# Sample attention of a two-layer streaming encoder: probability rows ordered by batch, cached products of 64 columns, sink values picked by one-hot constants

## The chip, the cores and the metric

The kernel runs on one core of one Trainium2 chip. The metric is the device time in microseconds (us) of one execution of the whole program. The kernel before was run three times; the profile is of one further execution. Engines carry the profile's names: PE is the matrix engine (PEld its weight loads), DVE the vector engine, ACT the scalar engine, POOL the general-purpose one, and SP the one whose queue issues most of the DMAs.

## The reference

One step of an encoder of two layers. Layer 0 ("mixer A") attends to a sliding window of its own keys, with a distance penalty (ALiBi) and one learned "sink" value for each head; layer 1 ("mixer B") attends to shared keys and values with a learned bias by relative distance, and no sink. After each attention comes an MLP of width 4096 with a squared ReLU. There are 1024 prompt tokens, and 8 running streams ("batches") of 16 new tokens each, the sample: its tokens attend to a cache of 128 keys of their own batch, and to the 16 new tokens of their own batch. 16 heads of 64 elements share 4 key/value heads (kv heads), so 4 query heads go to each kv head. Everything is float32.

```python
def attend(q, k, v, bias, sink):
    b, tq = q.shape[:2]
    qg = q.reshape(b, tq, N_KV_HEADS, GROUP, HEAD_DIM)
    s = jnp.einsum('bqhgd,bkhd->bhgqk', qg, k).astype(jnp.float32) * (HEAD_DIM ** -0.5)
    s = s + bias.reshape(N_KV_HEADS, GROUP, tq, -1)
    if sink is None:
        p = jax.nn.softmax(s, axis=-1)
    else:
        sk = sink.astype(jnp.float32).reshape(N_KV_HEADS, GROUP, 1, 1)
        m = jnp.maximum(jnp.max(s, axis=-1, keepdims=True), sk)
        e = jnp.exp(s - m)
        p = e / (jnp.sum(e, axis=-1, keepdims=True) + jnp.exp(sk - m))
    o = jnp.einsum('bhgqk,bkhd->bqhgd', p.astype(v.dtype), v)
    return o.reshape(b, tq, N_HEADS * HEAD_DIM)
...
as_ = attend(qs, k_all, v_all, alibi_bias(pos_s, kpos_a, slopes), sink_a[i])  # sample, layer 0
hs = hs + as_ @ w_o_a[i]
...
as_ = attend(qs, kb_all, vb_all, relpos_bias(pos_s, kpos_b, rel_bias_b[j]), None)  # sample, layer 1
hs = hs + as_ @ w_o_b[j]
```

## The kernel before, in words

**Tiles and stages.** The prompt is 8 tiles of 128 tokens, and the 8 x 16 sample tokens are a ninth tile (ST). Each layer runs as attention, output projection, up projection, down projection. On the profile of before these are, roughly: attention A and its output projection from 0 to 460 us, the MLP of layer 0 to 1150, attention B and its output projection to 1660, the MLP of layer 1 to the end. Most large products are made of three matmuls on a high and a low part of each operand (lines 147 to 149, 186 to 188, 715 to 717: the same operation three times).

**What sets the order.** The program is written as generators that are woven together (`weave`), and a scheduler then lays out each engine's instructions by a model of their lengths and dependences. So an edit in one place can move instructions in others. Each engine works its own list in order; an instruction that waits holds up all behind it. SP's DMAs take eight semaphores in rotation (DMAHW0 to DMAHW7): a DMA waits for the landing of the one that stands eight before it in the queue, as the waits in the order rows below show.

**The sample's attention.** `unit` (L506 to L590) does it for two batches (`bp`, 4 pairs) and one kv head (`j`, 4): 16 units in each layer, 32 in all, stepped at its `yield`s between pieces of the prompt's attention. A unit loads the caches (`kc` L509, `vc` L511), turns the keys (`ps_utr`, L544, copied by L545), forms scores for 128 rows (4 heads x 2 batches x 16 tokens, ordered head, batch, token) over 256 cached and 32 new columns, and exponentiates them. A row needs only the 128 cached columns of its own batch; the 128 of the other batch are masked by the bias, so their probabilities are zero. Then:
- ACT scales the 256 cached columns by 1/sum in place (L570, tile `sp` in layer A, `ub` in layer B) and the 32 new ones into `pn` (L571), a tile with 128 columns, zero elsewhere.
- PE turns three blocks of 128x128 (L574, L575 and L576 for `pn`, into `ps_utp`), and ACT copies all three to `pts` (L578).
- PE forms `ps_uo` = values x probabilities with 128 columns each: L582 and L583 for the two caches, L584 for the new tokens' values. These are plain float32 products, each of which stands as two instructions on PE.
- ACT copies `ps_uo` out in two halves (L587), and a DMA stores them.

`q_stage2` (L211) lays out the queries: for ST in the row order of the units. `prep_bias` (L1100) lays out layer B's biases for the units in the same row order, and `shape_constants` (L48) the constants of layer A, made on the host and passed in as `consts` (`cst`, 596 columns).

**The sinks.** `sinks` (L1239) runs at the start: it loads `cst` (L1242) and the sinks broadcast to all partitions (`sink` L1244, 128x16), forms `usink` from them (L1246, L1247), and then loads `ssink`, 128 rows x 4 kv heads, by four DMAs (L1251), each of which fetches 4 single elements, 4 apart, for 32 partitions. `ssink` and `susink`, made from it, are read first by the units of layer A.

**The start.** Weights of the first projection (`w_qkv_a`) come in pieces called `raw`, 128x2x512, through L129 in `load_block`; POOL (L156) and DVE (L159) split a piece into its high and low part `w`. PE's first projections (L186 to L188) follow them, and ACT (L245, L252, L253) and DVE (L246) empty their banks.

Of the kernel before, what the change touches and what calls it, by code (L numbers as in the profile page):

```python
# [8 lines left out]
F32 = mybir.dt.float32  # L9
# [7 lines left out]
P = 128  # L17
# [26 lines left out]
C_SLS = 592  # L44
C_W = 596


def shape_constants():  # L48
# [9 lines left out]
    for hh in range(4):  # L58
        for b in range(2):
            r = slice(hh * 32 + b * 16, hh * 32 + b * 16 + 16)  # L60
            sa[r, b * P : (b + 1) * P] = P + i[:, None] - np.arange(P)[None, :]
            sa[r, 256 + b * 16 : 256 + b * 16 + 16] = np.abs(i[:, None] - i[None, :])
# [4 lines left out]
    c[:, C_ISL : C_ISL + H] = 1.0 / s  # L67
    c[:, C_SLS : C_SLS + KV] = s.reshape(KV, G).T[np.arange(P) // 32]
    return c
# [6 lines left out]
class Build:  # L76
# [134 lines left out]
    def q_stage2(self, qpool, qr, t):  # L211
        pt = self.transpose_pairs(qr, 4)
        qT = qpool.tile([P, 2, G, P], F32R, tag="qT", name="qT", bufs=2)
        if t == ST:
            for j in range(2):
                src = pt[:, 2 * j : 2 * j + 2, :].rearrange("p h (b q) -> p h b q", b=4)
                dst = qT[:, j].rearrange("p h q -> p (h q)")
                dst = dst.rearrange("p (b h q) -> p h b q", b=4, h=G)
                self.stack(src, dst[:, 0::2], dst[:, 1::2])
        else:  # L220
            dst = qT.rearrange("p j h q -> p (j h) q")
            self.stack(pt, dst[:, 0::2], dst[:, 1::2])
        return [qT[:, 0], qT[:, 1]]
# [282 lines left out]
    def unit(self, up, small, layer, bp, j, v8, gq8, cache_k, cache_v):  # L506
# [58 lines left out]
        else:  # L565
# [3 lines left out]
            self.mark = nc.vector.reciprocal(li, l)  # L569
        nc.scalar.activation(p[:, 0:256], p[:, 0:256], AF.Copy, scale=li)  # L570
        nc.scalar.activation(pn[:, bp * 32 : bp * 32 + 32], p[:, 256:288], AF.Copy, scale=li)  # L571
        yield
        pt2 = self.psum("u", [P, 3, P], "ps_utp")
        nc.tensor.transpose(pt2[:, 0, :], p[:, 0:128], self.ident)  # L574
        nc.tensor.transpose(pt2[:, 1, :], p[:, 128:256], self.ident)  # L575
        nc.tensor.transpose(pt2[:, 2, :], pn, self.ident)  # L576
        pts = up.tile([P, 3, P], F32, tag="pts", name="pts")
        nc.scalar.copy(pts, pt2)  # L578
        yield
        po = self.psum("u", [64, 2, 2, 32], "ps_uo")  # L580
        pof = po.rearrange("p a b q -> p (a b q)")
        nc.tensor.matmul(pof, vc[:, 0, :], pts[:, 0, :], start=True, stop=False)  # L582
        nc.tensor.matmul(pof, vc[:, 1, :], pts[:, 1, :], start=False, stop=False)  # L583
        nc.tensor.matmul(pof, v8[:, j * HD : j * HD + HD], pts[:, 2, :], start=False, stop=True)  # L584
        so = up.tile([P, 2, 32], F32, tag="so", name="so")
        for par in range(2):
            nc.scalar.copy(so[par * 64 : par * 64 + 64], po[:, :, par, :])  # L587
        nc.sync.dma_start(
# [511 lines left out]
    def prep_bias(self, dp):  # L1100
        nc = self.nc
        with ExitStack() as st:
# [20 lines left out]
            for h4 in range(G):  # L1123
                for b in range(2):
                    r = slice(h4 * 32 + b * 16, h4 * 32 + b * 16 + 16)
                    nc.sync.dma_start(big[r, :, b * P : b * P + P], fsrc(h4, 0, 16, KV, G, P))
# [112 lines left out]
    def sinks(self, ring):  # L1239
# [8 lines left out]
        self.ssink = ring.tile([P, KV], F32, tag="ssink", name="ssink")  # L1248
        sk = I["sink_a"][0]
        for i in range(G):  # L1250
            nc.sync.dma_start(  # L1251
                self.ssink[i * 32 : i * 32 + 32, :],
                sk[i : i + 13 : 4].partition_broadcast(32),
            )
        self.nslope = ring.tile([P, KV], F32, tag="nslope", name="nslope")
# [543 lines left out]
```

## Time and profile before

| what | us |
|---|---|
| three runs | 2401.32, 2404.04, 2399.53 |
| median | 2401.32 |
| span of the profiled execution | 2399.3 |
| attention A, 0 to 430: PE busy | 397.20 of 430 |
| up projection of layer 0, 430 to 810: PE busy | 372.66 of 380 |
| attention B, 1150 to 1660: PE busy | 487.25 of 510 |

The profiled execution is known by its span; its whole time is not given apart from it. It stands 2.0 us under the median and 0.2 under the lowest of the three runs.

The table's PE figures are busy time between two points of the span, at the clock that was granted. The matmul records of PE overlap: the time from one's start to the next one's start is shorter than what a record gives as its duration. Where the length of PE's stream matters, the pieces of the chain of waits (start to start) are the ones to use. A row of the chain "389.63 0.11 PE ps_utp L575" reads: at 389.63 us from the span's start, 0.11 us, PE, the tile written, the line.

### The profile page before, as it was taken

Reading aid. Unit: us, or ns where it says so; the run is one execution under the profiler, and the core shown is the slowest. Engines: PE = TensorE matmul, PEld = TensorE weight load, DVE = VectorE, ACT = ScalarE, POOL = GpSimd, SP = SyncE. Lnnn points to the kernel's source line nnn. Section 1 sums busy time; section 2 is a strip of 40 time slices with the busy share of each in tenths; the row PEclk is TensorE's granted clock in tenths of the full one; section 3 lists DMA queues with packets and bytes.
Section 4 is the critical chain, followed back from the end, with each engine's and each line's share of the span. In section 5 each row is a group of like instructions: output and inputs, shape, how many; then the busy total and the mean of one; then the engine's idle time right before and its main releaser. Section 6 shows DMA issues by size and latency. Waiting matters only on the chain.

```text
span 2399.3 us, 33421 instructions
## 1 busy us (share of the span) xinstructions
PE 2320.4 (97%) x11621; PEld 1935.5 (81%) x11621; DVE 1626.3 (68%) x3002; ACT 1217.9 (51%) x2423; POOL 535.6 (22%) x828
## 2 busy tenths in 40 slices
PE   7998999899999999999999999998999999999999
PEld 6786877788888888888777788887888888888887
DVE  6687786755655777776567877877655555776674
ACT  4676675555555433232267666665655555333321
POOL 3343332312112100000333434344211211000000
PEclk9998999999999999999999999999999999999999
DMA  7345546244433874342743555555434435744332
GB/s 244 122 127 168 171 156 200 95 155 158 145 128 141 323 245 146 117 141 99 237 149 111 188 161 173 173 169 174 138 127 145 154 137 200 278 140 158 112 116 114
DMA packets 218457, 385.88 MB, mean 161 GB/s; under 512 B 50408, under 2 KB 125104, under 8 KB 211120
## 3 DMA queue, kind: packets, MB, share of 16 engines
q1 hardware_dynamic: 195136, 307.16, 39.0%
q0 software_dynamic: 21776, 71.84, 7.7%
q10 hardware_dynamic: 1376, 4.74, 0.5%
q8 instruction: 92, 1.51, 0.3%
q14 instruction: 77, 0.63, 0.1%
HBM read 246.47 MB, written 136.14 MB: 159 GB/s over the span
## 4 chain that ended last, share of the span: by engine, by line
PE 82%; DMA 7%; DVE 5%; ACT 2%; issue 2%; POOL 1%; SPq 1%; ACTq 0%; DVEq 0%; POOLq 0%
PE ps_x L715 9%; PE ps_x L717 9%; PE ps_x L716 9%; PE ps_y L717 7%; PE ps_y L716 7%; PE ps_y L715 7%; PE ps_mm L186 3%; PE ps_mm L188 3%; PE ps_mm L187 3%; PE ps_tr L293 2%; PE ps_mm L147 2%; PE ps_mm L149 2%; PE ps_mm L148 2%; PE ps_s L717 1%; PE ps_s L716 1%
## 5 line engine op out<-in xcount | busy, mean ns | idle before, releaser
L109 ACT CAST w<-r 128x2048 fp32r<-128x2048 f32 x56 | 107.1, 1913 | 322.9 <-PE ps_y L717 212.1
L715 PE MATMUL ps_x<-w,s 128*128 128x512 f32 x512 | 199.5, 390 | 2.7 <-DVE hc L854 2.1
L717 PE MATMUL ps_x<-w,s 128*128 128x512 f32 x512 | 199.4, 389 | 0.0
L716 PE MATMUL ps_x<-w,s 128*128 128x512 f32 x512 | 199.2, 389 | 0.0
L186 PE MATMUL ps_mm<-w,hh 128*128 128x512 f32 x432 | 175.0, 407 | 13.8 <-ACT kw L253 5.1
L188 PE MATMUL ps_mm<-w,hl 128*128 128x512 f32 x432 | 174.3, 403 | 1.7 <-DMA hl<-hTd 1.4
L187 PE MATMUL ps_mm<-w,hh 128*128 128x512 f32 x432 | 172.5, 400 | 0.7 <-DVE w L159 0.7
L109 ACT CAST s<-s 128x2048 fp32r<-128x2048 f32 x56 | 107.1, 1913 | 117.9 <-DMA s<-hd 108.6
L115 DVE TENSOR_TENSOR w<-r,w 128x2048 fp32r<-128x2048 f32 x56 | 128.2, 2290 | 51.9 <-ACT w L109 51.9
L715 PE MATMUL ps_x<-sx,w 128*128 128x512 f32 (+1 forms) x408 | 157.8, 387 | 4.6 <-ACT hc L834 2.7
L1021 DVE TENSOR_TENSOR x<-ps_y,x 128x512 f32<-128x512 f32 x136 | 92.3, 687 | 101.1 <-PE ps_y L717 101.0
L717 PE MATMUL ps_x<-sx,w 128*128 128x512 f32 (+1 forms) x408 | 154.1, 378 | 0.0
L716 PE MATMUL ps_x<-sx,w 128*128 128x512 f32 (+1 forms) x408 | 154.1, 378 | 0.0
L109 ACT CAST w<-ru 128x512 fp32r<-128x512 f32 (+1 forms) x160 | 110.0, 708 | 85.3 <-PE ps_y L716 32.0
L717 PE MATMUL ps_y<-w,s 128*128 128x512 f32 x384 | 149.5, 389 | 0.0
L716 PE MATMUL ps_y<-w,s 128*128 128x512 f32 x384 | 149.4, 389 | 0.0
L715 PE MATMUL ps_y<-w,s 128*128 128x512 f32 x384 | 149.4, 389 | 0.0
L115 DVE TENSOR_TENSOR s<-s 128x2048 fp32r<-128x2048 f32 x56 | 128.1, 2287 | 26.5 <-ACT s L109 26.5
L115 DVE TENSOR_TENSOR ptl<-ps_tr,pth 128x512 fp32r<-128x512 f32 x180 | 122.6, 685 | 24.8 <-ACT pth L109 19.0
L115 DVE TENSOR_TENSOR w<-ru,w 128x512 fp32r<-128x512 f32 (+1 forms) x160 | 126.6, 793 | 10.9 <-ACT w L109 10.8
L109 ACT CAST pth<-ps_tr 128x512 fp32r<-128x512 f32 x180 | 104.8, 594 | 47.9 <-PE ps_tr L293 39.3
L115 DVE TENSOR_TENSOR wq<-ru,wq 128x1024 fp32r<-128x1024 f32 x32 | 39.7, 1240 | 131.9 <-ACT wq L109 131.9
(280 smaller groups left out, 6573.3 us busy)
## 6 DMA issues: line engine op xcount, KB each, us to landing
s<-hd SPq DMA_DIRECT2D x56, 1024.0 KB, 4.7
ru<-in_w_up SPq DMA_DIRECT2D x64, 512.0 KB, 3.9
r<-in_w_down SPq DMA_DIRECT2D x32, 1024.0 KB, 5.7
hd<-hc POOLq DMA_DIRECT2D x128, 256.0 KB, 2.7
hd<-hs POOLq DMA_DIRECT2D x96, 256.0 KB, 2.5
x<-xd SPq DMA_DIRECT2D x41, 512.0 KB, 4.6
o<-oTd SPq DMA_DIRECT2D x52, 256.0 KB, 4.1
hTd<-hh SPq DMA_DIRECT2D x36, 256.0 KB, 4.5
```

What stands on the lines that cost most here:

```text
L109: a = nc.scalar.copy(hi, src)
L115: return a, e.tensor_tensor(lo, src, hi.bitcast(F32), ALU.subtract)
L147: nc.tensor.matmul(ps, oh[:, k, :], w[:, 0, k, nn], start=(k == 0), stop=False)
L148: nc.tensor.matmul(ps, oh[:, k, :], w[:, 1, k, nn], start=False, stop=False)
L149: nc.tensor.matmul(ps, ol[:, k, :], w[:, 0, k, nn], start=False, stop=(k == 3))
L186: nc.tensor.matmul(ps, a, w[:, 0, k, :], start=(k == 0), stop=False)
L187: nc.tensor.matmul(ps, a, w[:, 1, k, :], start=False, stop=False)
L188: nc.tensor.matmul(ps, b, w[:, 0, k, :], start=False, stop=(k == KC - 1))
L715: a = mm(ps, ah, bh, start=first, stop=False, skip_group_check=True)
L716: mm(ps, ah, bl, start=False, stop=False, skip_group_check=True)
L717: return a, mm(ps, al, bh, start=False, stop=last, skip_group_check=True)
L1021: tt(xs[t][:, N[n]], ps, xs[t][:, N[n]], ALU.add)
```

## The change

In `unit` the 128 rows are ordered batch, head, token, so that each batch has 64 rows in a row. The probabilities of the cached columns of both batches then go into the same 128 columns: batch 0's rows keep columns 0 to 127, and for batch 1's rows the columns 128 to 255 are written into 0 to 127, by the scaling, which is two instructions of 64 rows x 128 columns in place of one of 128 x 256. There are two blocks to turn in place of three, `pts` has 256 columns in place of 384, and each cache's product has 64 columns in place of 128, into its own half of `ps_uo`. The product of the new tokens stands first and opens the bank. The copies out of `ps_uo` undo the new row order, so the stored output is laid out as before. The layouts of queries, biases and constants follow. The four DMAs of `ssink` go; four small DVE instructions form it from `sink` and four one-hot columns added to `cst` (600 columns).

```diff
@@ shape_constants
-            r = slice(hh * 32 + b * 16, hh * 32 + b * 16 + 16)
+            r = slice(b * 64 + hh * 16, b * 64 + hh * 16 + 16)
...
-    c[:, C_SLS : C_SLS + KV] = s.reshape(KV, G).T[np.arange(P) // 32]
+    c[:, C_SLS : C_SLS + KV] = s.reshape(KV, G).T[np.arange(P) % 64 // 16]
+    c[:, C_OH : C_OH + G] = np.arange(P)[:, None] % 64 // 16 == np.arange(G)
@@ q_stage2, sample tile
-                src = pt[:, 2 * j : 2 * j + 2, :].rearrange("p h (b q) -> p h b q", b=4)
+                src = pt[:, 2 * j : 2 * j + 2, :].rearrange("p h (b q) -> p h b q", b=8)
                 dst = qT[:, j].rearrange("p h q -> p (h q)")
-                dst = dst.rearrange("p (b h q) -> p h b q", b=4, h=G)
+                dst = dst.rearrange("p (b h q) -> p h b q", b=8, h=G)
@@ unit
-        nc.scalar.activation(p[:, 0:256], p[:, 0:256], AF.Copy, scale=li)
+        for b in range(2):
+            r = slice(b * 64, b * 64 + 64)
+            nc.scalar.activation(p[r, 0:P], p[r, b * P : b * P + P], AF.Copy, scale=li[r])
         nc.scalar.activation(pn[:, bp * 32 : bp * 32 + 32], p[:, 256:288], AF.Copy, scale=li)
         yield
-        pt2 = self.psum("u", [P, 3, P], "ps_utp")
-        nc.tensor.transpose(pt2[:, 0, :], p[:, 0:128], self.ident)
-        nc.tensor.transpose(pt2[:, 1, :], p[:, 128:256], self.ident)
-        nc.tensor.transpose(pt2[:, 2, :], pn, self.ident)
-        pts = up.tile([P, 3, P], F32, tag="pts", name="pts")
+        pt2 = self.psum("u", [P, 2, P], "ps_utp")
+        nc.tensor.transpose(pt2[:, 0, :], p[:, 0:P], self.ident)
+        nc.tensor.transpose(pt2[:, 1, :], pn, self.ident)
+        pts = up.tile([P, 2, P], F32, tag="pts", name="pts")
         nc.scalar.copy(pts, pt2)
         yield
-        po = self.psum("u", [64, 2, 2, 32], "ps_uo")
-        pof = po.rearrange("p a b q -> p (a b q)")
-        nc.tensor.matmul(pof, vc[:, 0, :], pts[:, 0, :], start=True, stop=False)
-        nc.tensor.matmul(pof, vc[:, 1, :], pts[:, 1, :], start=False, stop=False)
-        nc.tensor.matmul(pof, v8[:, j * HD : j * HD + HD], pts[:, 2, :], start=False, stop=True)
+        po = self.psum("u", [64, P], "ps_uo")
+        nc.tensor.matmul(
+            po, v8[:, j * HD : j * HD + HD], pts[:, 1], start=True, stop=False,
+            skip_group_check=True,
+        )
+        for b in range(2):
+            c = slice(b * 64, b * 64 + 64)
+            nc.tensor.matmul(
+                po[:, c], vc[:, b, :], pts[:, 0, c], start=False, stop=(b == 1),
+                skip_group_check=True,
+            )
         so = up.tile([P, 2, 32], F32, tag="so", name="so")
+        pv = po.rearrange("p (b a r q) -> p r a b q", b=2, a=2, r=2)
         for par in range(2):
-            nc.scalar.copy(so[par * 64 : par * 64 + 64], po[:, :, par, :])
+            d = so[par * 64 : par * 64 + 64].rearrange("p a (b q) -> p a b q", b=2)
+            nc.scalar.copy(d, pv[:, par])
@@ prep_bias
-                    r = slice(h4 * 32 + b * 16, h4 * 32 + b * 16 + 16)
+                    r = slice(b * 64 + h4 * 16, b * 64 + h4 * 16 + 16)
@@ sinks
-        sk = I["sink_a"][0]
         for i in range(G):
-            nc.sync.dma_start(
-                self.ssink[i * 32 : i * 32 + 32, :],
-                sk[i : i + 13 : 4].partition_broadcast(32),
-            )
+            oh, sv = self.cst[:, C_OH + i : C_OH + i + 1], self.sink[:, i : H : G]
+            if i == 0:
+                nc.vector.tensor_scalar(self.ssink, sv, oh, None, ALU.mult)
+            else:
+                nc.vector.scalar_tensor_tensor(self.ssink, sv, oh, self.ssink, ALU.mult, ALU.add)
```

The lists of instructions of the two programs differ so: PE has 11495 in place of 11527, ACT 2081 in place of 2049, DVE 3008 in place of 3004, SP 976 DMAs in place of 980, and POOL 833 in both. Line numbers after stand 2 higher in most of the file, 11 higher behind `unit`.

**The start, on SP's queue.** The rows below are the DMAs of SP behind the load of `cst`, in the program before, each with the semaphores that it waits for. `raw` is a piece of `w_qkv_a`, `x` a tile of the prompt, `kc` and `vc` the caches of the first unit.

```order
L1244 DMA sink<-in_sink_a 128x16 [waits DMAHW2_49]
L1251 DMA ssink<-in_sink_a 32x4x1 [waits DMAHW3_49]
L1251 DMA ssink<-in_sink_a 32x4x1 [waits DMAHW4_49]
L1251 DMA ssink<-in_sink_a 32x4x1 [waits DMAHW5_49]
L1251 DMA ssink<-in_sink_a 32x4x1 [waits DMAHW6_49]
L129 DMA raw<-in_w_qkv_a 128x2x512 [waits DMAHW7_49,DVE_49]
L129 DMA raw_359<-in_w_qkv_a 128x2x512 [waits DMAHW0_49,DVE_49]
L1319 DMA x<-in_x_prompt 128x1024 [waits DMAHW1_49,PE_49]
L1319 DMA x<-in_x_prompt 128x1024 [waits DMAHW2_49,PE_49]
L509 DMA kc<-in_cache_k_a 128x2x64 [waits DMAHW3_49]
L511 DMA vc<-in_cache_v_a 128x2x64 [waits DMAHW4_49]
L129 DMA raw<-in_w_qkv_a 128x2x512 [waits DMAHW5_49,DVE_49]
```

In the changed program the same place reads:

```order
L1255 DMA sink<-in_sink_a 128x16 [waits DMAHW2_49]
L131 DMA raw<-in_w_qkv_a 128x2x512 [waits DMAHW3_49,DVE_49]
L1330 DMA x<-in_x_prompt 128x1024 [waits DMAHW4_49,PE_49]
L1330 DMA x<-in_x_prompt 128x1024 [waits DMAHW5_49,PE_49,Activation_49]
L511 DMA kc<-in_cache_k_a 128x2x64 [waits DMAHW6_49]
L513 DMA vc<-in_cache_v_a 128x2x64 [waits DMAHW7_49]
L131 DMA raw_359<-in_w_qkv_a 128x2x512 [waits DMAHW0_49,DVE_49]
L1675 DMA gb<-in_g_mlp 128x1024 [waits DMAHW1_49]
L131 DMA raw<-in_w_qkv_a 128x2x512 [waits DMAHW2_49,DVE_49]
L131 DMA raw_371<-in_w_qkv_a 128x2x512 [waits DMAHW3_49,DVE_49]
```

Without the four `ssink` loads the first `raw` and the two `x` stand four places further ahead; the second piece, `raw_359`, has moved behind `kc` and `vc`, and `gb` ahead of the third piece. Before, `gb` and `raw_371` stood right behind the rows shown.

**A unit on PE.** The rows are PE's in the first unit of layer A, from the scores of a prompt tile (`ps_s`) to the unit's products, before. `ps_pv`, `ps_tr` and `ps_n` belong to the prompt.

```order
L349 MATMUL ps_s<-KT,qT 128x256 x8
L574 MATMUL ps_utp<-identr,sp 128x128
L575 MATMUL ps_utp<-identr,sp 128x128
L293 MATMUL ps_tr<-identr,p 128x128 x4
L576 MATMUL ps_utp<-identr,pn 128x128
L300 MATMUL ps_pv<-pth,VS 128x512
L179 MATMUL ps_n<-identr,x 128x128 x8
L301 MATMUL ps_pv<-ptl,VS 128x512
L582 MATMUL ps_uo<-pts,vc 64x128
L583 MATMUL ps_uo<-pts,vc 64x128
L584 MATMUL ps_uo<-pts,v_216 64x128
```

The changed program has at this place:

```order
L351 MATMUL ps_s<-KT,qT 128x256 x8
L578 MATMUL ps_utp<-identr,sp 128x128
L295 MATMUL ps_tr<-identr,p 128x128 x4
L579 MATMUL ps_utp<-identr,pn 128x128
L302 MATMUL ps_pv<-pth,VS 128x512
L181 MATMUL ps_n<-identr,x 128x128 x8
L303 MATMUL ps_pv<-ptl,VS 128x512
L584 MATMUL ps_uo<-pts,v_216 64x128
L590 MATMUL ps_uo<-pts,vc 64x64 x2
```

One transpose is gone, the new tokens' product stands first, and the two cached products have 64 columns; the prompt's rows around them stay where they were.

**A unit on ACT, near the loads of W_o.** The rows are ACT's at a unit late in attention A, before: `w` are pieces of the output projection's weights (L109 is the line of every high-part cast), `pth` the prompt's turned probabilities, for which PE's `ps_pv` waits.

```order
L570 ACTIVATE sp<-sp,li 128x256
L571 ACTIVATE pn<-sp,li 128x32
L195 ACTIVATE qn<-ps_mm 128x512
L196 COPY qr<-ps_mm 128x512
L109 CAST w<-raw 128x1024
L109 CAST w<-raw_4730 128x1024
L109 CAST w<-raw_4948 128x1024
L109 CAST pth<-ps_tr 128x512
L578 COPY pts<-ps_utp 128x384
```

And in the changed program:

```order
L574 ACTIVATE sp<-sp,li 64x128 x2
L575 ACTIVATE pn<-sp,li 128x32
L197 ACTIVATE qn<-ps_mm 128x512
L198 COPY qr<-ps_mm 128x512
L111 CAST w<-raw 128x1024
L111 CAST w<-raw_4730 128x1024
L111 CAST w<-raw_4948 128x1024
L111 CAST pth<-ps_tr 128x512
L111 CAST oh<-o 128x512
L581 COPY pts<-ps_utp 128x256
```

The scaling is two instructions, the copy to `pts` is shorter and has moved behind the cast `oh`; the three casts of `w` stay ahead of `pth`. In attention A the lists of the engines are otherwise changed in places; in attention B instructions have moved broadly on ACT, DVE and PE; in the MLPs the lists are the same.

3 lines of the change are left out of this document (2 added, 1 removed).

## The prediction

> **What bounds the kernel now.** I read the page's busy shares first, then the chain of waits, then busy time by stage.
>
> ```profile
> PE 2320.4 (97%) x11621; PEld 1935.5 (81%) x11621; DVE 1626.3 (68%) x3002; ACT 1217.9 (51%) x2423; POOL 535.6 (22%) x828
> PE 82%; DMA 7%; DVE 5%; ACT 2%; issue 2%; POOL 1%; SPq 1%; ACTq 0%; DVEq 0%; POOLq 0%
> ```
>
> PE is busy 97% of the span and holds 82% of the chain: what shortens PE's stream can shorten the whole, except where PE stands and waits. The stages in which the units run, and the start (columns: stretch, length, busy time of PE, PEld, DVE, ACT, POOL with instructions, granted clock, DMA share, GB/s):
>
> ```profile
> 15.00:18.50 3.50, 3.50 (x17) 2.90 (x16) 3.50 (x12) 2.44 (x5) 0.00 (x0) 1.00 0.08 9
> 18.50:28.50 10.00, 9.97 (x44) 7.91 (x43) 4.84 (x6) 0.95 (x2) 5.04 (x7) 1.00 0.99 368
> 28.47:32.48 4.01, 0.00 (x1) 0.03 (x1) 2.69 (x4) 0.76 (x3) 2.55 (x4) 0.96 1.05 404
> 32.48:35.76 3.28, 3.28 (x8) 2.61 (x9) 2.32 (x5) 0.26 (x1) 1.01 (x2) 0.53 1.05 391
> 0.00:430.00 430.00, 397.20 (x2084) 328.00 (x2085) 321.02 (x947) 270.16 (x744) 155.16 (x265) 0.97 0.52 169
> 1150.00:1660.00 510.00, 487.25 (x2627) 401.81 (x2626) 375.57 (x1006) 315.31 (x856) 211.20 (x280) 1.00 0.55 172
> ```
>
> In attention A PE is busy 92%, in attention B 96%. ACT, on which the units also lean, has 63% and 62%. One large hole lies at the start: PE stands from 28.47 to 32.48 and then runs 3.28 us at a clock of 0.53. Just ahead of it the DMA engines carry 9 GB/s from 15.0 to 18.5. SP's queue in that time (start, length, what, count) and the chain out of the hole:
>
> ```profile
> 11.95 2.30 SPq L1251 DMA_DIRECT2D ssink<-in_sink_a  x4
> 14.37 1.05 SPq L129 DMA_DIRECT2D raw<-in_w_qkv_a  x2
> 15.82 1.84 SPq L1319 DMA_DIRECT2D x<-in_x_prompt  x2
> ...
> 19.23 0.52 SPq L129 DMA_DIRECT2D raw<-in_w_qkv_a  x1
> ```
> ```profile
> 19.23 9.41 DMA raw<-in_w_qkv_a
> ...
> 28.73 0.70 POOL w L156
> 29.46 1.83 DVE w L159 x2
> 31.29 0.41 DVE VS L246
> ...
> 31.99 0.40 ACT kw L253
> ...
> 32.48 0.77 PE ps_mm L186
> 33.24 0.43 PE ps_mm L187
> ...
> 35.76 0.23 PE ps_mm L187
> ```
>
> The third piece of `raw`, issued at 19.23, lands at 28.64. DVE stands at its split (L159) and only then empties a bank (L246), for which PE waits through ACT's L253. The four `ssink` loads hold SP's issue for 2.42 us (11.95 to 14.37). They also stand ahead of `raw`, issued at 14.37, in a stretch where the DMA engines move next to nothing: I read this as single elements trickling through the queues. 3.5 us at 9 of some 370 GB/s are about 3.4 us of lost transfer.
>
> **The start, part by part.** Without these loads the order puts `raw` at 11.95 and the third piece some 3 us earlier (one `x`, `kc`, `vc` and `gb` still ahead of it). Of the hole of 4.01 us, 2.42 us is the least that goes (issue alone), and all of it the most. I take 3.4, the lost transfer: ACT's copies of the banks (L245, then L252 and L253 in turn) end about 0.6 us behind PE's last product whatever DVE does, so 0.6 us of hole stays. The clock: eight products run at a pitch of 0.43 instead of 0.23, 8 x 0.20 = 1.6 us; with PE standing 0.6 us I count that as gained (nothing to 1.6). So the start gives **5.0 us** (2.4 to 5.6). Behind it the same engines are late again by less: the fourth piece's split on DVE, covered by PE's products on the third.
>
> The clock drop behind the hole bears on a page of the Trainium skill, "TensorE: Matmul & The Clock Gate", section "Part 1: The HAM clock gate": the clock halves after an idle window of some 3.4 us and comes back after as much busy time. By that rule a hole of 0.6 us drops nothing, and one of 1.6 (issue alone) drops nothing either, so the least would be 4.0 rather than 2.4. The trace agrees with the length of the cold stretch here (3.28 us).
>
> The four DVE instructions that make `ssink` anew cost little: the nearest are `usink`'s at 128x16.
>
> ```profile
> L1247 DVE TENSOR_SCALAR usink<-usink x1: 165/165/165, 18.3 to 18.3; 128x16 f32<-128x16 f32 x1
> ```
>
> 4 x 0.165 = 0.66 us, on a DVE that is full from 15.0 to 18.5 but busy only 4.84 of the next 10 us; hidden there, and 0.7 us if that cover goes.
>
> **A unit on PE.** Pieces of the chain are start to start, so they add up:
>
> ```profile
> 389.63 0.11 PE ps_utp L575
> 389.74 0.11 PE ps_utp L576
> ...
> 392.61 0.36 PE ps_uo L582 x2
> 392.97 0.22 PE ps_uo L583 x2
> 393.19 0.22 PE ps_uo L584 x2
> ```
> ```profile
> 194.35 0.10 PE ps_utr L544 x2
> L583 PEld LDWEIGHTS ps_uo<-pts,vc x64: 133/137/137, 96.2 to 1643.7; 128*64 128x64 f32 x64
> ```
>
> One transpose less is 0.11 us. A float32 product of 128 columns takes 0.22 us, two instructions of 0.11. Half the columns at the same rate are 0.056 each, so the two cached products fall from 0.44 to 0.22 us. No product of 64 columns stands in the trace; the bounds are no gain at all (pitch 0.11) and half. I take half: PE issues L544, also with a weight load each, at 0.05. Saved per unit 0.11 + 0.22 = 0.33, times 32 units **10.5 us** of PE's stream (3.5 if 64 columns are no faster than 128).
>
> Not all of it reaches the end. PE is the bound for 92 to 96% of these stages; but a product that comes sooner sometimes only waits longer for softmax work on ACT and DVE. Between all of it and half I take three quarters: **7.9 us** (5 to 10.5).
>
> On the same spacing the Trainium skill's page "TensorE: Matmul & The Clock Gate", section "Back-to-back issue gap", speaks against the gain: pairs of weight load and matmul settle at about 81 ns for 128 columns, above the plain column rate. An estimate from it: four instructions would fall from 109 to 81 ns, 0.11 us a unit in place of 0.22. The trace's L544 pairs at 0.05 each go against it, in a train of only two.
>
> **A unit on ACT.** ACT now makes two scalings where it made one, and a shorter copy:
>
> ```profile
> L570 ACT ACTIVATE sp<-sp,li x16: 496/510/532, 89.9 to 388.7; 128x256 f32<-128x256 f32 x16
> L571 ACT ACTIVATE pn<-sp,li x16: 304/307/332, 90.3 to 389.2; 128x32 f32<-128x32 f32 x16
> L578 ACT COPY pts<-ps_utp x32: 477/483/524, 94.3 to 1642.3; 128x384 f32<-128x384 f32 x32
> L545 ACT CAST kb<-ps_utr x32: 362/376/420, 82.4 to 1633.3; 128x256 fp32r<-128x256 f32 x32
> ```
>
> From 32 columns (307 ns) to 256 (510 ns) a column costs 0.91 ns, so 128 columns take 307 + 96 x 0.91 = 394 ns, and two 788: 0.28 us later at the transposes. The copy falls from 483 to some 376 (the cast of 256 columns). ACT's own sum grows by 0.28 - 0.11 = 0.17 us a unit, 5.5 us in all, on an engine idle over a third of these stages. What counts is the delay of the first transpose. The lists of PE's waits, of attention A and of attention B (what waited, for what, us in total, times, the longest):
>
> ```profile
> PE ps_utp L574 <- ACT sp L570: 1.4, 3, 0.6
> PE ps_utp L574 <- ACT ub L570: 0.3, 1, 0.3
> ```
>
> Four of 32 units wait there (1.4 and 0.3 us). Four times 0.28 is 1.1 us; PE's prompt products cover the others, and without that cover it is 32 x 0.28 = 9 us. I take **1.0**.
>
> At nothing go the stores, the queries' and biases' layouts (the same elements in the same number of instructions and DMAs) and the copies of `ps_uo` (64 columns per row as before). They are bounded by 0.1 us a unit either way, 3 us, on ACT and not on PE.
>
> **The sum.** 2399.3 - 5.0 - 7.9 + 1.0 = 2387.4 us for the profiled execution, which stands 2.0 under the median of the runs; so **2389.4 us** for the median, 11.9 us (0.5%) faster. About 0.2%, 4.8 us, is what a measurement of this kernel can tell from no change: faster means under 2396.5, slower over 2406.1.
>
> **The rivals.**
> - *The PE gain is swallowed.* Attention B's order moves broadly, and PE's gaps take up what its stream gives. Then the start's gain alone is left: 2401.3 - 5.0 = 2396.3. For it: PE waits for some 7% of attention A already. Against it: in attention B it waits 4%.
> - *The start keeps its hole.* `raw_359` now stands behind both `x`, `kc` and `vc`, and POOL's cast of `kc` may hold its split; if DVE meets the same lateness at the second piece, the start gains nothing: 2401.3 - 7.9 + 1.0 = 2394.4. Against it: `raw_359`'s place in the queue is the same in number, its four `ssink` predecessors gone.
> - *Products of 64 columns are no faster than those of 128*, because a weight load (137 ns a row above) goes with each and the spacing does not fall below 0.11. Then 3.5 x 3/4 = 2.6 is left of PE's gain: 2401.3 - 5.0 - 2.6 + 1.0 = 2394.7. It is the direction of the page's spacing rule, though further than its 81 ns.
> - *ACT's longer scaling delays the prompt's casts* `pth` (L109), for which PE's `ps_pv` (L300) waits, and the clock falls behind such a wait. This is the slower case; the trace has one such place (from attention A's waits, ACT's timeline and the busy time by stretch):
>
> ```profile
> PE ps_pv L300 <- ACT pth L109: 5.4, 4, 2.3
> 337.81 2.95 ACT L109 CAST w<-raw 128x1024 fp32r<-128x1024 f32 x3
> 342.78:349.60 6.82, 6.12 (x24) 5.03 (x23) 6.49 (x15) 5.51 (x16) 1.68 (x3) 0.50 0.47 134
> ```
>
> There PE waits 2.3 us behind three casts of `w`, and then has half its clock for 6.82 us, 3.4 us lost: 5.7 us in all. In attention B, where the order is new, one such wait takes most of the start's gain; two new ones with the PE gain swallowed give 2401.3 - 5.0 + 11.4 = 2407.7, and with the PE gain kept it takes three (2406.5). Two or three decide. Against it: three heavy casts together stand only where W_o is loaded, and ACT is idle 38% of attention B.
>
> **Chances.** Forecast 0.43; PE gain swallowed 0.17 (0.04 faster, 0.13 the same); hole kept 0.13 (0.10, 0.03); no faster at 64 columns 0.15 (0.13, 0.02); ACT's delay 0.12, slower. So faster 0.70, the same 0.18, slower 0.12. The range: the most is 5.6 + 10.5 with no cost on ACT, 2385.2, and a wait less with its cold stretch (some 4 us) 2381. Upwards it takes in the first three rivals and an ACT cost of 9 us in place of 1.0 (2397.4), with one wait of 5.7 more 2403; 2404 leaves out the slower case.
>
> **What would show it.** Right: `raw` issued near 12 us, no stretch of 9 GB/s, PE's hole near 29 us under 1 us and no half clock behind it; the two cached products at 0.11 us a pair in the chain and two transposes per unit; PE's busy time some 10 us less in attention A and B together. Wrong: a hole of several us at the second or third piece; pairs of 64 columns at 0.2; new waits of `ps_pv` for `pth` over 2 us in attention B followed by a granted clock of half; the W_o phase of either layer later by more than its attention gained.

## The result, and the profile after

| | median us | lowest to highest | ratio to before, 95% |
|---|---|---|---|
| before, 20 runs beside the changed kernel | 2403.91 | 2399.53 to 2411.05 | |
| changed, 20 runs | 2412.77 | 2404.62 to 2419.22 | 1.0028 (1.0019 to 1.0038) |

The change makes the kernel slower, by 0.28% or 6.7 us by the ratio; the two medians stand 8.9 us apart. The forecast was 11.9 us faster. The profiled execution after took 2405.47 us, with a span of 2403.7, at the low end of its runs, so its trace shows less of the loss than the medians do. A run's time stands 1.8 us above its span, so the profiled execution of before, with a span of 2399.3, was a run of some 2401.1 us, like the median of the three runs: the 2.0 us between them is the step from span to time. Of all executions only one, of e1_sinks below, fell far out (6904.39 us); the ratio of e1_sinks leaves it out. The first lines of the page after, and the engines' shares of the chain:

```profile
span 2403.7 us, 33364 instructions
...
PE 2315.2 (96%) x11589; PEld 1928.8 (80%) x11589; DVE 1625.8 (68%) x3006; ACT 1226.2 (51%) x2455; POOL 537.1 (22%) x828
...
PE 79%; DMA 7%; DVE 6%; ACT 4%; issue 2%; POOL 1%; SPq 1%; ACTq 0%; DVEq 0%; POOLq 0%
```

PE is busy 5.2 us less in all, and yet the span is 4.4 us longer: PE's share of the chain fell from 82 to 79%, and DVE and ACT took it, 6 and 4% in place of 5 and 2. Stretches of the start and of attention B (the columns of the prediction):

```profile
15.00:18.50 3.50, 3.50 (x17) 2.89 (x16) 2.08 (x9) 2.06 (x4) 0.00 (x0) 1.00 0.96 374
...
29.40:30.10 0.70, 0.13 (x2) 0.09 (x1) 0.70 (x2) 0.70 (x3) 0.01 (x1) 1.00 0.99 380
30.10:33.50 3.40, 3.40 (x15) 2.81 (x16) 2.19 (x6) 0.20 (x1) 1.02 (x1) 1.00 0.93 342
...
1150.00:1660.00 510.00, 478.21 (x2547) 392.40 (x2548) 367.46 (x991) 315.88 (x865) 204.58 (x273) 0.98 0.54 167
1338.00:1341.70 3.70, 1.35 (x6) 0.83 (x6) 3.62 (x14) 3.29 (x10) 2.20 (x2) 1.00 0.79 245
1341.70:1345.00 3.30, 3.10 (x7) 2.03 (x8) 2.99 (x9) 1.81 (x6) 1.91 (x3) 0.50 0.89 259
...
1352.00:1355.00 3.00, 0.83 (x6) 0.40 (x5) 0.59 (x1) 1.67 (x3) 0.00 (x0) 1.00 0.79 291
1355.00:1361.00 6.00, 5.75 (x22) 3.92 (x21) 5.84 (x13) 4.54 (x10) 0.00 (x0) 0.53 0.70 210
```

At the start the stretch of 9 GB/s is gone (374), PE stands only for 0.57 us near 29.5, and its clock is 1.00 behind that. In attention B it is the other way round: PE is busy 478.21 of 510 us where it was 487.25, and the granted clock over the stretch fell from 1.00 to 0.98. These two windows are the same in time, but the stage has moved. From the last `ps_x` of layer 0 to the first of layer 1 it lasted 506.8 us before (1166.2 to 1673.0) and lasts 522.7 us after (1155.0 to 1677.7). So the changed kernel is 11.2 us ahead where the stage begins, and loses 15.9 us in it. The last rows show one place of that loss: PE stands for 2.35 us of the 3.70 from 1338.0, and for 2.17 of the 3.00 from 1352, and behind each of the two stretches the clock is half, 0.50 and 0.53.

The start's chain, where the hole of 4.01 us was:

```profile
17.65 8.10 DMA raw<-in_w_qkv_a
...
25.82 0.73 POOL w L158
...
26.58 2.17 DVE w L161 x2
...
28.77 0.48 DVE VS L248
...
30.04 0.47 PE ps_mm L188
30.50 0.23 PE ps_mm L189
```

The third piece, issued at 17.65, lands 8.10 us later at 25.75, in place of 28.64. PE still stands briefly ahead of 30.04 (0.57 us, from the end of its product before at 29.47), and its products run on at 0.23 us.

A unit's products in the chain, in attention A, and its instructions on ACT (the view of one line: shortest, median and longest duration in ns, then the first and last start):

```profile
92.01 0.36 PE ps_uo L584 x2
92.37 0.23 PE ps_uo L590 x4
```
```profile
L574 ACT ACTIVATE sp<-sp,li x32: 393/400/410, 85.3 to 378.0; 64x128 f32<-64x128 f32 x32
L581 ACT COPY pts<-ps_utp x32: 353/377/428, 90.2 to 1644.5; 128x256 f32<-128x256 f32 x32
```

The three products stood as 0.36 + 0.22 + 0.22 = 0.80 us before and are 0.36 + 0.23 = 0.59 now; four instructions of 64 columns take 0.058 us each. The scaling of 64x128 takes 400 ns (forecast 394), the copy 377 (forecast 376).

What PE waits for, in attention A for the scaling, and then in attention B for the scaling, the copy `pts` and the rows `hh` that the projections read (total, times, longest):

```profile
PE ps_utp L578 <- ACT sp L574: 5.2, 4, 2.7
```
```profile
PE ps_utp L578 <- ACT ub L574: 2.7, 3, 1.7
...
PE ps_uo L584 <- ACT pts L581: 2.4, 2, 2.2
PE ps_mm L188 <- DMA hh<-hTd: 1.9, 2, 1.7
```

Each part of the unit thus came out near the forecast, and yet the whole is slower. Two causes can be told apart by runs: the new *unit* costs more in attention B than its rows say, or the new *order* of attention B does, which the scheduler made because the unit's lengths changed.

### The profile page after: what moved, and what is told of

Its sections match the earlier page's. It is cut to its first block, busy times and chain, and to the rows that moved or that the text cites. A ratio compares the mean times of both kernels' runs of the same rounds, so it can differ in the third digit from the quotient of the medians.

```text
span 2403.7 us, 33364 instructions
## 1 busy us (share of the span) xinstructions
PE 2315.2 (96%) x11589; PEld 1928.8 (80%) x11589; DVE 1625.8 (68%) x3006; ACT 1226.2 (51%) x2455; POOL 537.1 (22%) x828
## 4 chain that ended last, share of the span: by engine, by line
PE 79%; DMA 7%; DVE 6%; ACT 4%; issue 2%; POOL 1%; SPq 1%; ACTq 0%; DVEq 0%; POOLq 0%
PE ps_x L726 10%; PE ps_x L728 9%; PE ps_x L727 9%; PE ps_y L726 7%; PE ps_y L728 7%; PE ps_y L727 7%; PE ps_mm L188 3%; PE ps_mm L190 3%; PE ps_mm L189 3%; PE ps_tr L295 2%; PE ps_mm L149 1%; PE ps_mm L150 1%; PE ps_mm L151 1%; PE ps_s L728 1%; PE ps_s L727 1%
```

## The experiments

Ratios are to runs of the kernel before made beside them on the same chip; 0.1% is 2.4 us.

**One part at a time.** Three kernels take the change apart. A pair of flags says in which layer the unit and its row order are new; the sinks by one-hot constants are in all three.

```diff
+NEW = (False, False)   # e1_sinks;  (True, False): e2_unit_a;  (False, True): e3_unit_b
...
-        for b in range(2):
+        if NEW[layer]:
+          for b in range(2):
...
+        else:
+            nc.scalar.activation(p[:, 0:256], p[:, 0:256], AF.Copy, scale=li)
```

> Only the sinks by one-hot constants; the units and their row order as before, and every engine's order as before but for a few rows at the start. Both theories: the four loads of single elements go, the hole of PE near 28.5 us shrinks from 4.0 to under 1 us, the whole is 4 to 5 us shorter (ratio 0.998). If the hole stays, no change.

> The sinks and the new unit in layer A alone; attention B's instructions and their order are those of before. Theory 1 (the loss is made by the new order in attention B): 10 to 12 us shorter than before (ratio 0.9955), since attention A keeps the 11 us it gained in the changed kernel and B loses nothing. Theory 2 (the unit itself, its longer scaling on ACT, is what costs): the units of layer A cost too, less than 4 us beyond the sinks' gain is left or it is lost later.

> The sinks and the new unit in layer B alone; attention A as before. The scheduler gives attention B an order that is neither that of before nor that of the changed kernel. Theory 1 (order): attention B comes out anywhere from 5 us shorter to 15 us longer than before, and its gaps stand at other places than in the changed kernel. Theory 2 (the unit itself): attention B loses some 15 us again, so about 10 us longer than before in all, at the same kind of wait (PE for the unit's scaling and copy on ACT).

| | median us | ratio, 95% | attention B's order |
|---|---|---|---|
| e1_sinks | 2396.25 | 0.9981 (0.9970 to 0.9992) | as before |
| e2_unit_a | 2388.14 | 0.9945 (0.9930 to 0.9959) | as before |
| e3_unit_b | 2407.64 | 1.0027 (1.0015 to 1.0040) | a third one |

The sinks give 0.19%, and the unit in layer A 0.36% more. With both the kernel is 0.55% faster than before, so the loss is made by the unit in layer B, or by what comes with it. That e3's order is neither the old nor the changed kernel's leaves the two causes together.

**Order and unit apart.** The lists of instructions can be held. For each engine the wanted order is read from another build of the same program, and each instruction then gets a dependence on the one ahead of it on its own engine, which orders the two and waits for nothing. e4 has the whole change in the order of e2; e5 has e2's program (old unit in layer B) in the order of the changed kernel. Set beside each other in the traces, the engines' lists of e5 and the changed kernel differ in attention B in no row but the unit's own, and so do those of e4 and e2. Those of before and the changed kernel differ widely: of some 2,570 rows of PE there, the unit's left out, 1,702 stand in an order that both have, and about a third does not.

```diff
+    _, _, order = build(inputs, [True, False])           # e5: [True, True]
+    nc, arrays, _ = build(inputs, [True, True], order)   # e5: [True, False]
...
+                for a, b in zip(seq, seq[1:]):
+                    tc.add_manual_dep(b, a.name, AFTER, reason="order")
```

> All of the change, with every engine's order in attention B held to the order of before (that of the run with the new unit in layer A alone). Theory 1 (the new order costs): attention B now gains too, some 3 to 5 us beyond the run with layer A alone, so 15 to 17 us shorter than before (ratio 0.9935). Theory 2 (the new unit itself costs in attention B): about as long as the changed kernel, ratio 1.002 to 1.004.

> Sinks and layer A as changed; in layer B the old unit (one scaling, three transposes, products of 128 columns), but every engine held to the order that the changed kernel has there. Theory 1 (order): the loss stays, 12 to 20 us longer than the run with layer A alone, ratio to before 1.000 to 1.004. Theory 2 (the unit itself): as short as the run with layer A alone, ratio 0.9945.

| | unit in B | order of B | median us | ratio, 95% |
|---|---|---|---|---|
| e2_unit_a | old | old | 2388.14 | 0.9945 (0.9930 to 0.9959) |
| e4_new_unit_old_order | new | old | 2388.70 | 0.9951 (0.9937 to 0.9965) |
| e12_old_order_again (e4 once more) | new | old | 2388.08 | 0.9950 (0.9935 to 0.9965) |
| e5_old_unit_new_order | old | new | 2407.88 | 1.0032 (1.0020 to 1.0043) |
| changed | new | new | 2412.77 | 1.0028 (1.0019 to 1.0038) |

> The run with the whole change in the old order once more, for the comparison with the second scaling on POOL (0.9938 in the call before) under the same state of the chip. If POOL's share of the scaling gained, this stays at 0.995; if it did not, this comes to 0.994.

This settles it. The order of attention B costs 0.77 to 0.87% (18 to 21 us), with either unit; the unit in B alone makes no difference that these runs can tell, in either order. The traces agree: the stage lasts 505.6 us in e2, 507.9 and 504.1 in e4 and e12, and 523.3 in e5, beside 522.7 in the changed kernel. The busy time of e4 over attention B, with the rows around W_o's loads, and then the rows around the loads of the changed kernel and of e5:

```profile
1150.00:1660.00 510.00, 482.87 (x2595) 398.25 (x2593) 382.05 (x1008) 321.85 (x878) 210.84 (x280) 0.99 0.55 170
1297.00:1369.00 72.00, 68.35 (x365) 54.75 (x365) 63.55 (x165) 52.45 (x142) 31.86 (x38) 1.00 0.59 180
1345.00:1369.00 24.00, 22.80 (x123) 17.87 (x122) 21.66 (x54) 18.60 (x48) 10.15 (x11) 1.00 0.74 231
```
```profile
1297.00:1369.00 72.00, 63.64 (x322) 50.58 (x321) 54.42 (x141) 46.47 (x124) 27.69 (x34) 0.93 0.48 152
1345.00:1369.00 24.00, 21.41 (x101) 16.75 (x100) 13.02 (x28) 13.35 (x31) 5.76 (x8) 0.86 0.57 187
```
```profile
1297.00:1369.00 72.00, 63.21 (x319) 50.53 (x318) 54.59 (x142) 46.22 (x123) 26.20 (x33) 0.93 0.49 150
```

In the 72 us around the loads PE does 365 instructions in the old order and 322 and 319 in the new one, at a clock of 1.00 and 0.93. Every engine is less busy there (DVE 54.42 us in place of 63.55), so none of them has more work: they wait for one another or for DMAs. How far the stage has fallen behind is read from PE's scores of the units (the view of one line, the first and last start), of the changed kernel and of e4:

```profile
L551 PE MATMUL ps_us<-kb,qu x28: 288/294/377, 1271.1 to 1640.6; 128*128 128x288 f32 x28
```
```profile
L552 PE MATMUL ps_us<-kb,qu x28: 292/295/403, 1270.8 to 1626.8; 128*128 128x288 f32 x28
```

Level to 0.3 us at 1271, 13.8 us apart at the last.

**Where in the order?** In the new order the four loads of W_o (`raw` from `w_o_b`) stand in a row on SP. SP's timeline around 1330 to 1360, changed kernel and then e4:

```profile
1342.33 9.00 SPq L140 DMA_DIRECT2D raw<-in_w_o_b  x4
...
1356.08 0.38 SPq L1369 DMA_DIRECT2D hh<-hTd  x1
```
```profile
1337.10 0.33 SPq L141 DMA_DIRECT2D raw<-in_w_o_b  x1
...
1341.07 0.55 SPq L141 DMA_DIRECT2D raw<-in_w_o_b  x1
...
1345.14 0.33 SPq L1395 DMA_DIRECT2D hh<-hTd  x1
1345.56 0.38 SPq L1395 DMA_DIRECT2D hl<-hTd  x1
1346.03 2.19 SPq L141 DMA_DIRECT2D raw<-in_w_o_b  x2
```

Four loads in a row hold SP for 9.00 us, and the next `hh` is issued at 1356.08. On ACT, in the changed kernel, the casts of these pieces wait for them, and the copy `pts` stands behind the third cast:

```profile
1347.48 2.24 ACT L111 CAST w<-raw 128x1024 fp32r<-128x1024 f32 x2 [1.14 <-DMA raw<-in_w_o_b]
1353.33 1.04 ACT L111 CAST w<-raw 128x1024 fp32r<-128x1024 f32 x1 [3.62 <-DMA raw<-in_w_o_b]
1354.29 0.37 ACT L581 COPY pts<-ps_utp 128x256 f32<-128x256 f32 x1
```

PE's timeline has the two waits that end the gaps of the stretches above (in brackets the idle time ahead of the row, and what ended it):

```profile
1341.83 0.76 PE L188 MATMUL ps_mm<-w,hh 128*128 128x512 f32 x1 [1.69 <-DMA hh<-hTd]
...
1354.70 0.43 PE L584 MATMUL ps_uo<-pts,v 128*64 128x128 f32 x2 [2.17 <-ACT pts L581]
```

The first is 1.69 us for `hh`, the second 2.17 us for the copy `pts`. The `hh` of the first wait had been issued at 1337.46, ahead of the four loads, so these did not make it; for the `hh` issued at 1356.08 PE waits only 0.17 us here. I tried the suspects in turn.

*SP's order of two `w_q_b` loads.* They stand ahead of the unit's `qu` and `kb` in the new order and behind in the old. e6 puts the new seven places into the old order, e7 the old ones into the new order; e8 does e7 with 35 places.

```diff
+    sp = order["EngineType.SP"]
+    sp[584:591] = sorted(sp[584:591], key=place.get)   # e8: sp[580:615]
```

> The whole change with attention B in the order of before, as the last run but one, but for seven places of SP's queue near 1330 us: the two pieces of w_q_b stand ahead of the loads of the unit's queries and keys (qu, kb), as in the changed kernel. Theory SP (the second piece waits for its buffer, and behind it qu, kb and the prompt's hh and hl come late, PE waits for hh and falls to half clock): 6 to 11 us longer than the run with all of the old order, ratio to before 0.998 to 1.000. Rival (the order on PE, ACT and DVE costs, not the queue): as that run, ratio 0.995.

> The whole change in its own new order, but for the same seven places of SP's queue: the two pieces of w_q_b stand again behind qu and kb. Theory SP: the waits of PE near 1340 us for hh and the half clock behind them go, 6 to 11 us shorter than the changed kernel, ratio to before 0.998 to 1.000. Rival: as the changed kernel, ratio 1.003.

> As the run before this one, with SP's places 580 to 614 in the relative order of before, so the four pieces of w_o_b too stand again behind the loads of hh, hl and the bias. Theory SP: a further 1 to 4 us shorter (the waits near 1352 us go too), ratio to before 0.997 to 0.9985. Rival: as the changed kernel, ratio 1.003.

e6: 2391.08, 0.9958 (0.9943 to 0.9973). e7: 2414.77, 1.0065 (1.0048 to 1.0083). e8: 2429.09, 1.0120 (1.0105 to 1.0135). The suspect falls: the pieces' new places do no harm that shows in the old order, and the old places do not heal the new one. SP's queue taken back alone makes it worse, and PE's waits from 1297 to 1400 show why (e7, then e8):

```profile
PE ps_tr L296 <- POOL p L453: 8.3, 2, 8.0
PE ps_uo L588 <- ACT pts L585: 3.7, 1, 3.7
```
```profile
PE ps_uo L588 <- ACT pts L585: 11.4, 1, 11.4
PE ps_tr L296 <- POOL p L453: 8.3, 2, 8.0
```

The loads now come later than the lists of POOL and ACT count on. In e7 POOL stands 14.96 us for a piece of `w_q_b` that `p` stands behind; in e8 ACT stands 5.75, 2.45 and 4.58 us for pieces of `w_o_b` that `pts` stands behind. The queues of one order fit each other; one queue from another order is a new wait.

*Where the loss is made.* e9 follows the changed kernel up to a cut and the old order behind it. In the traces its lists part from the changed kernel's at 1392 us on ACT, 1394 on DVE and 1398 on PE, later than the 1368 of its expectation.

```diff
+CUT = {'PE': 6660, 'Activation': 1316, 'DVE': 1752, 'Pool': 540, 'SP': 616}
+        order[e] = first[e][:c] + then[e][c:]
```

> The whole change; every engine keeps the changed kernel's order in attention B up to a cut near 1368 us (between the sixth and the seventh unit of layer B), and has the order of before behind it. Theory place (most of the loss is made between 1320 and 1361 us, where the new order's waits of PE and the half clock behind them stand): 9 to 13 us longer than the run with all of the old order, ratio to before 0.999 to 1.001. Rival (the loss is spread over the whole of attention B): 3 to 6 us longer, ratio 0.9965 to 0.9975.

2409.18, 1.0019 (1.0004 to 1.0033): more than the theory gave, and most of the loss stays with the old order behind the cut. So it is made ahead of the cut, or at the seam. The traces tell more. Equal work is counted here in columns of PE's products since the last `ps_x` of layer 0. At equal work the changed kernel, against e12, is 1.6 us behind at 1337 us, 10.3 at 1365, 9.4 at 1388, 15.9 at 1431, and 18.6 at the end of the stage. About half is thus lost between 1337 and 1365, where the two waits above stand. e9 is 10.2 us behind at its 1393 and 16.5 at 1411, so its next 6 us fall at the seam, and where the changed kernel loses the rest is not settled by it.

*The casts of W_o ahead of the copy.* e11 keeps the new order but for ACT's four casts and DVE's four low parts of these pieces, which go some places later, behind the copy `pts`.

```diff
+MOVES = {'Activation': [(1262, 1266), (1263, 1268), (1264, 1270), (1267, 1272)],
+         'DVE': [(1683, 1686), (1684, 1686), (1685, 1692), (1689, 1695)]}
```

> The whole change in its own new order, but near 1347 us ACT's four casts of pieces of w_o_b and DVE's four low parts of them stand a few places later, so that the unit's copy to pts and the prompt's casts pth no longer stand behind casts that wait for their DMA. Theory (in the new order ACT and DVE stand at weight pieces that have not landed, with the work that PE waits for behind them): PE's wait of 2.2 us for pts near 1354 us goes and the half clock there is shorter, 2 to 6 us shorter than the changed kernel, ratio to before 1.0005 to 1.002. Rival (it is the lateness from before 1341 us alone): as the changed kernel, 1.003.

2413.46, 1.0054 (1.0036 to 1.0072): no gain. The wait for `pts` is gone from PE's list, and others stand in its place. From 1297 to 1400, and SP's timeline:

```profile
PE ps_mm L189 <- DMA hh<-hTd: 4.6, 2, 2.7
PE ps_pv L303 <- ACT pth L112: 3.0, 1, 3.0
```
```profile
1342.74 12.64 SPq L141 DMA_DIRECT2D raw<-in_w_o_b  x4
...
1359.73 0.38 SPq L1395 DMA_DIRECT2D hh<-hTd  x1
```

The later casts free the `raw` buffers later: SP's four loads wait 5.8 us for DVE's low parts in place of 3.1, so they hold SP for 12.64 us in place of 9.00. `hh` is issued at 1359.73, and PE waits 2.65 us for it. In this place the casts and SP's row of loads are one knot: with the one end loosened, the other tightened.

*The second half of w_q_b.* e13 puts its pieces (loads on SP, splits on POOL and DVE, 23 rows) behind their old neighbours in the new order.

```diff
+            order[e] = carry(order[e], like[e], pieces[n][e])   # n is 0
```

> The whole change in its own new order, but every instruction of the second half of w_q_b (its loads on SP, its high parts on POOL, its low parts on DVE; 23 rows in all) stands in layer B behind the neighbour that it has in the order of before. Theory (the early places of these pieces hold up SP's queue and DVE at the start of the loss): the waits of PE before 1342 us shrink, 4 to 10 us shorter than the changed kernel, ratio to before 0.999 to 1.0015. Rival (the order of PE, ACT and DVE among themselves is what costs, the weight pieces only ride along): as the changed kernel or longer, 1.003 or more.

2418.64, 1.0065 (1.0041 to 1.0089), with a wait of 6.1 us for `hh`: it falls too. The same for the pieces of W_o, loads, casts and low parts together, was not run.

**Which engine's order decides?** e14 holds only PE's list, in the order of e2 (attention B as before), and leaves the other four to the scheduler; e15 holds only SP's.

```diff
-PINNED = [f"EngineType.{e}" for e in ("PE", "Activation", "DVE", "Pool", "SP")]
+PINNED = [f"EngineType.{e}" for e in ("PE",)]   # e15: ("SP",)
```

> The whole change; of the five engines PE alone is held to its order of before, the others are the scheduler's, and come out nearly as before (some 160 rows moved, in the changed kernel some 1,900). Theory (PE's order in attention B, with what the scheduler builds round it, is enough): as the run with all five held, ratio 0.995. Rival (the few moved rows on DVE, ACT and SP carry the loss): 1.000 or more.

> The whole change with SP's queue alone held to its order of before; the scheduler then gives the engines an order that is neither that of before nor that of the changed kernel (PE has 1,534 rows moved against before, 1,412 against the changed kernel). Theory (the order of before is better than what the scheduler finds for another cost of the unit, SP's queue is not the cause): ratio 0.999 to 1.004, as the two other new orders. Rival (SP's queue carries the loss): 0.995 to 0.997.

e14: 2393.31, 0.9953 (0.9937 to 0.9969). e15: 2399.47, 0.9980 (0.9970 to 0.9991), with a fourth order on PE. Holding PE's list is enough: some 160 rows still move on the other engines, and the ratio is e4's. Holding SP's gets some three fifths of the way from the changed kernel's 1.0028 to e4's 0.9951, between what was expected for theory and for rival. In the changed kernel some 1,900 rows move, so holding PE's list brings nearly the whole order back. That shows where the order can be held; that PE's list alone does the harm, with the other lists as they are in the changed kernel, is not shown.

**Why does the unit in B bring nothing?** In the old order PE's stream is shorter by the same amount per unit as in layer A, and yet e4 is no faster than e2. One suspect is ACT's second scaling; e10 puts it on POOL in layer B.

```diff
-                a = nc.scalar.activation(p[r, 0:P], p[r, b * P : b * P + P], AF.Copy, scale=li[r])
+                if b and layer:
+                    a = nc.gpsimd.tensor_scalar(p[r, 0:P], p[r, b * P : b * P + P], li[r], 1.0, ALU.mult, ALU.mult)
```

> As the run with the whole change in the old order, but in layer B the second scaling of a unit is done by POOL beside ACT's first one, so the transposes no longer wait for two scalings in a row. Theory ACT (the gain on PE's stream in attention B is eaten by the longer scaling on ACT): 3 to 6 us shorter than that run, ratio to before 0.9925 to 0.994. Rival (PE in attention B is held by other work of DVE and ACT, so that a shorter unit moves nothing): the same, ratio 0.995.

2389.11, 0.9938 (0.9927 to 0.9950), against 0.9951 and 0.9950 of e4 and e12: the ratio lies where the theory put it, but the intervals overlap and the medians do not differ (2388.70 and 2388.08 there), so no gain is shown. The traces speak against the suspect: in attention B of e4 PE waits for the scaling only 0.6 us in all (0.3 in e2), and in e10 4.1 us, now for POOL. What takes up the unit's 5 us in layer B stays open.

## Why the prediction was wrong

- **The start: right.** `raw` was issued at 11.95 us, the 9 GB/s are gone, the hole is 0.57 us (0.6 forecast) with no half clock behind it. e1 gives 0.19% (0.08 to 0.30), 4.6 us, against 5.0; in its trace the hole is 1.1 us. The Trainium skill's rule on the page "TensorE: Matmul & The Clock Gate", section "Part 1: The HAM clock gate", by which a hole so short drops nothing, agrees with this one. It does not agree with attention B, where PE's longest gaps of 1.69 and 2.17 us are shorter than the rule's 3.4 and half clock follows all the same.
- **A unit on PE: right in size.** 0.21 us in the products and 0.11 for the transpose are 0.32, against 0.33. PE's busy time, which was to fall by some 10 us, fell by 5.2, but it is a poor sign: at half clock a record of the same product is longer (0.63 us at 1342.40, 0.39 at 1345.27). The Trainium skill's page "TensorE: Matmul & The Clock Gate", section "Back-to-back issue gap", gives some 81 ns for 128 columns; the prediction's estimate from it, 81 ns as the least for 64 columns too, does not hold here, where they run at 58 ns. In layer A e2 gained 0.36% over e1, some 8.6 us where 16 units hold 5.1 (their two traces reach layer 0's first `ps_x` at 432.1 and 429.2 us); the two intervals are 0.11 and 0.15% to each side, so that more than 5.1 came is not shown.
- **A unit on ACT: right per instruction, low in its waits.** PE waits 5.2 us for the scaling in attention A in place of 1.4, and 2.7 in attention B in place of 0.3. That is 6.2 us more where 1.0 was taken. In the old order it is 4.0 us (5.1 and 0.6 us in e4); and e2, with its 5.1 us of such waits in attention A, gains 0.36% there, so no such cost shows on the path.
- **"I take three quarters: 7.9 us": the step that failed.** It spread PE's 10.5 us evenly over both layers and took the stream as all that changes. Layer A gave its share. Layer B gave nothing in the old order (e4 against e2), and the new order took 18 to 21 us. The prediction saw that order: it spoke of PE's gaps taking up the gain, "Attention B's order moves broadly", and so let the new order lose no more than the unit gained. It had no term for an order that is worse by itself. With the measured ratios the sum is: sinks -0.19%, unit in A -0.36%, unit in B +0.06% (none that can be told from zero), order of B +0.77%, together +0.28%. It closes by construction, since each term is the step from one run's ratio to the next.
- **The slower rival: near in form, wrong in cause.** It put the loss in attention B at casts of W_o that PE's work stands behind, with half the clock after it, and gave 2406.5 to 2407.7. So it looks: `pts` behind the cast of `w`, a PE wait of 2.17 us, clock 0.53. But its cause, ACT's longer scaling, is not the cause: with the old scaling in the new order (e5) the kernel is as slow, and with the new scaling in the old order (e4) as fast as e2. Its chance of 0.12 rested on ACT being idle enough, which says nothing on the order.
- **The clock.** Half clock is part of the loss. Over the timed runs the mean granted clock is 0.9894 in e5 and 0.9934 in e4, made beside each other. An estimate from these means: 0.0040 of some 2400 us is at most 10 us of the 19 between the two, since half clock costs time only where PE has work. The changed kernel's mean is 0.9894 as well. The rest would be time in which PE stands.
- **What stays open.** Which rows of the new order do the harm. About half of it is made between 1337 and 1365 us, it goes when PE's list is held (e14), and no small group of rows that I moved carries it.

e2, e4, e10, e12 and e14 are all faster than both kernels, at 0.9938 to 0.9953. The change keeps its worth if attention B's order is held, on PE alone if need be.

## What to carry to other kernels

Where a scheduler lays out the engines' lists from a model of lengths, an edit has two effects, its own and that of the new order, and the second can be several times the first: here 5 us of work less in a stage moved about a third of PE's rows there, and the new order cost 18 us. Price them apart: build the edit in the old order (order-only dependences along each engine's list, or along PE's alone) and the old code in the new order, before any row of the edit is tuned. When the forecast is made from durations and the lists show that a whole stage is laid out anew, the chance of a loss should come from that, not from the edit's own terms.

## What the runs showed of the hardware

- A float32 product of 64 columns, two instructions each with a weight load, runs at 0.058 us an instruction in a train of four: half of the 0.11 of 128 columns.
- Half the clock follows short gaps too. In the stretches of the changed kernel PE stands 2.35 of 3.7 us and then has 0.50 for 3.3 us; it stands 2.17 of 3.0 us and then has 0.53 for 6.0. The start's gap of 0.57 us cost nothing. The clock records of the changed kernel's trace hold nine stretches of half clock; but for the last, which the end cuts off, each lasts 3.41 us or two or three times that, and all begin on one grid of 3.41 us. From 7 us on, each step of the grid in which PE was busy 0.50 of the time or less was followed by half clock, and a step at full clock with 0.52 or more was not. In the traces of other runs half clock also followed some steps with up to 0.65, so this is no sharp threshold.
- Four loads in a row held SP for 9.00 us, and for 12.64 with their casts later; e4 issued the same four in 0.33, 0.55 and 2.19 us with other work between them. Of the 9.00 us, 3.1 are waits for DVE's low parts, which read the buffers, and 4.0 for the landing of another piece of W_o; of the 12.64 it is 5.8 and 4.0. Behind them in the queue stands a load (`hh`) that needs none of these.
